# FFN joints: the first pair's gate and up products taken in turns, the final norm's stores issued by POOL, the weights' sums in five buffers

## The chip, the cores and the metric

The kernel runs on one core of a Trainium2 chip. The metric is the device time of one execution in microseconds, the median of several runs. TensorE (PE in the profile) multiplies; VectorE (DVE), ScalarE (ACT) and GpSimd (POOL) do the elementwise work; SyncE (SP) issues transfers. Each engine runs its own instructions strictly in their order and waits on semaphores of the others.

## What is computed

An encoder block of width 1024 over 2048 tokens and 16 meta tokens: neighbourhood attention and a gated DeltaNet side by side, an output projection, then the feed-forward part (FFN) with 2816 hidden columns and a final norm. Only the last lines of the reference matter here:

```python
h = h + jnp.concatenate([y_na, y_dn], axis=-1) @ w_out[l]
u = rmsnorm(h, g_ffn[l])
h = h + (jax.nn.silu(u @ w_gate[l]) * (u @ w_up[l])) @ w_down[l]
...
return rmsnorm(h, g_final)[:, N_META:]
```

Everything is float32. On the chip each factor is split into a high and a low part (hi is the value rounded by a cast on ACT, lo the rest, subtracted on DVE), and a product is hi·hi + hi·lo + lo·hi.

## The kernel before, in words

All of the change lies in `phase_c`. Its first part (lines 1290 to 1434) multiplies by `w_out`, adds the residual, norms each of 16 token tiles and transposes it (`finish`, L1399). The FFN follows in two blocks of 1024 tokens. A block is `gate_up(blk)` and then `down(blk)`.

**Gate and up.** The hidden columns are taken in 11 pairs of column tiles. For each pair there are two rounds, n even for gate and n odd for up, so 22 rounds, and each is a 2 by 2 block product done in the seven products of Strassen and Winograd in place of eight. The right-hand operands of the seven, called by their roles, depend only on the tokens:

```python
    ROLES = ("B11", "T2", "T3", "T1", "B21", "T4", "B22")
    RESIDENT = 4
```

B11 to B22 are quarters of the block's transposed tokens, T1 to T4 sums of them made on POOL (L1416). The first four roles stay in SBUF (pool `u2`, called the residents below). The last three are written to DRAM (`S.ut`, name `ut`) and brought back when `gate_up` begins: `fetch` (L1454) loads each in two halves of 512 KB into the two raw buffers of pool `rawT` (name `rt`, L1451), and `hilo` (L1364) splits each half, ACT's cast at L1365 and DVE's subtraction at L1366. In block 1 the first of the three, B21, is loaded during `down(0)` already (`refill`, L1640).

The left-hand operands are the weights. `weights(n)` (L1461) loads two raw tiles (`rw`; pool `raw_a` for gate, `raw_b` for up), makes four sums s1 to s4 on POOL (name `s`, L1472, pool `sC` of four buffers) and splits seven operands into tiles of pool `w4C` (name `w4`, eight buffers). `gate_up` runs over

```python
            seq = [(n, i) for n in range(NFF) for i in range(7)]
```

with the operands prepared seven products ahead (`AHEAD`). A product is 12 matmuls of 128x512 (L1521) into a PSUM tile `pg`; DVE adds it out of PSUM to tiles `eg` (gate) or `eu` (up) at L1533, ACT applies silu to gate (L1537), and DVE multiplies by up and SP stores the result to `hd` (L1541, L1542). In block 0, `finish` of the last token tile runs inside `gate_up` (`before`, at i == 1): eight transposes (L1408), sums (L1416) and stores to `ut` (L1422).

**Down.** `down(blk)` (L1568) multiplies by `w_down` in two halves of four token tiles (L1593). At the end of a half, `leave(j)` (L1600) norms each tile: DVE adds the residual into `o` (L1607), ACT squares (L1608), DVE makes the reciprocal root (L58 to L64), ACT scales (L1612), POOL multiplies by the gain `gvec` (L1613) and SP stores 512 KB (L1614). The last half of all goes another way; the other three halves make 12 such stores.

A **joint** is the place where a block's `gate_up` begins: the first behind the `w_out` products, the second behind `down(0)`. The order on each engine is not the order of this code: a scheduler that simulates the program moves instructions forward and back within the limits of their data and buffers.

Of the kernel before, what the change touches and what calls it, by code (L numbers as in the profile page):

```python
# [8 lines left out]
F32 = mybir.dt.float32  # L9
# [3 lines left out]
ALU = mybir.AluOpType  # L13
# [3 lines left out]
P = 128  # L17
# [3 lines left out]
D = 1024  # L21
# [25 lines left out]
def bc(ap, shape):  # L47
    return ap.to_broadcast(shape)
# [1241 lines left out]
def phase_c(tc, S, W, wes, x, w_out, g_ffn, w_gate, w_up, w_down, g_final, out):  # L1290
# [6 lines left out]

    nc = tc.nc
    NFF = 22
    ROLES = ("B11", "T2", "T3", "T1", "B21", "T4", "B22")  # L1300
    RESIDENT = 4
    with ExitStack() as ps_es:
        es = ExitStack()
# [16 lines left out]
        pd_ = ps_es.enter_context(tc.tile_pool(name="pdC", bufs=2, side="right", space=PSUM))  # L1320
# [22 lines left out]
        yT, hs, us, bt = {}, {}, {}, {}  # L1343
# [16 lines left out]
        pg_ = ps_es.enter_context(tc.tile_pool(name="pgC", bufs=4, space=PSUM))  # L1360
# [38 lines left out]
        def finish(j, new):  # L1399

            u = us.pop(j)
            t = order[j]
            even = raw_t.tile([P, 2, 512], F32, name="rt") if t % 2 == 0 else None
            for hf in range(2):
                pt = pt_.tile([P, 4, P], F32, name="tp")
                for q in range(4):
                    k = hf * 4 + q
                    nc.tensor.transpose(pt[:, q], u[:, k * P:(k + 1) * P], S.ident)  # L1408
                b = even[:, hf].rearrange("p (q c) -> p q c", c=P) if t % 2 == 0 else new()
                nc.scalar.copy(b, pt)  # L1410
                bt[f"B{hf + 1}{t % 2 + 1}"] = b
            if t % 2 == 0:
                return
            for d, x0, x1 in (("T1", "B12", "B11"), ("T2", "B22", "T1"), ("T3", "B22", "B12"), ("T4", "B21", "T2")):
                bt[d] = new()
                nc.gpsimd.tensor_tensor(bt[d], bt[x0], bt[x1], ALU.subtract)  # L1416
            o = slice(t % 8 // 2 * P, (t % 8 // 2 + 1) * P)
            for i, r in enumerate(ROLES):
                if t < 8 and i < RESIDENT:
                    hilo(T[r][:, 0, :, o], T[r][:, 1, :, o], bt[r])  # L1420
                else:
                    nc.sync.dma_start(S.ut[t // 8, i, :, :, o], bt[r])  # L1422
            bt.clear()
# [12 lines left out]
        wes.close()  # L1436

        w4 = ps_es.enter_context(tc.tile_pool(name="w4C", bufs=8, side="right", reuse_waits="tile"))
        sp = ps_es.enter_context(tc.tile_pool(name="sC", bufs=4, side="right", reuse_waits="tile"))
        raw_b = ps_es.enter_context(tc.tile_pool(name="rawB", bufs=2, side="right", reuse_waits="tile"))  # L1440
        ev = ps_es.enter_context(tc.tile_pool(name="evC", bufs=7, side="right", reuse_waits="tile"))
        gl = ev.tile([P, D], F32, name="gvec", bufs=1)
        nc.sync.dma_start(gl, bc(g_final, [P, D]))

        ahead = {}

# [14 lines left out]
        def weights(n):  # L1461

            f, m = n // 2 * 2, n % 2
            raw = []
            for q in range(2):
                raw.append((raw_a, raw_b)[m].tile([P, KB, P], F32, name="rw"))
                nc.sync.dma_start(raw[q], (w_gate, w_up)[m][f + q])
            a11, a12, a21, a22 = (raw[i][:, 4 * j:4 * j + 4] for i in range(2) for j in range(2))

            def sum_(p, q, op):  # L1470
                s = sp.tile([P, 4, P], F32, name="s")
                nc.gpsimd.tensor_tensor(s, p, q, op)  # L1472
                return s

            def operand(src):
                w = w4.tile([P, 2, 4, P], F32R, name="w4")
                hilo(w[:, 0], w[:, 1], src)
                return w

            yield  # L1480
            s1 = sum_(a21, a22, ALU.add)
            s2 = sum_(s1, a11, ALU.subtract)
            yield operand(a11)
            yield operand(s2)
            s3 = sum_(a11, a21, ALU.subtract)
            s4 = sum_(a12, s2, ALU.subtract)
            yield operand(s3)
            yield operand(s1)
            yield operand(a12)
            yield operand(a22)  # L1490
            yield operand(s4)

        def gate_up(blk, before=None):


            AHEAD = 7
            gens = {n: weights(n) for n in range(NFF)}
            for n in range(2):
                next(gens[n])
            seq = [(n, i) for n in range(NFF) for i in range(7)]  # L1500
            made = {}

            def prepare(i):
                if i < len(seq):
                    n, p = seq[i]
                    made[i] = next(gens[n])
                    if p == 6 and n + 2 < NFF:
                        next(gens[n + 2])

            for i in range(AHEAD):  # L1510
                prepare(i)
            V = {}
            for i, (n, p) in enumerate(seq):
                if p == 0:
                    v = V[n % 2] = {}
                gate = n % 2 == 0
                ps = pg_.tile([P, 512], F32, name="pg")
                w, t = made.pop(i), T[ROLES[p]]
                for k in range(4):
                    for a, b in ((0, 0), (0, 1), (1, 0)):  # L1520
                        nc.tensor.matmul(ps, w[:, a, k], t[:, b, k], start=(k == 0 and (a, b) == (0, 0)), stop=(k == 3 and a == 1))  # L1521
                prepare(i + AHEAD)
                if i == 1:
                    if before:
                        before(lambda: ev.tile([P, 4, P], F32, name="eu", bufs=5) if len(bt) < 5 else ev.tile([P, 4, P], F32, name="eg"))
                    for r in ROLES[RESIDENT:]:
                        fetch(r, blk)

                def new():
                    return ev.tile([P, 512], F32, name="eg") if gate else ev.tile([P, 512], F32, name="eu", bufs=5)  # L1530

                def add(dst, x0):
                    nc.vector.tensor_tensor(dst, ps, x0, ALU.add)  # L1533

                def done(c, q, half):
                    if gate:
                        nc.scalar.activation(c, c, AF.Silu)  # L1537
                        V[q, half] = c
                    else:
                        h = V.pop((q, half))  # L1540
                        nc.vector.tensor_tensor(h, c, h, ALU.mult)  # L1541
                        nc.sync.dma_start(S.h[blk, n - 1 + q, :, half, :], h)  # L1542

                if p == 0:
                    v["u1"] = new()
                    nc.scalar.copy(v["u1"], ps)
                elif p == 1:
                    v["u2"] = new()
                    add(v["u2"], v["u1"])
                elif p == 2:  # L1550
                    v["u3"] = new()
                    add(v["u3"], v["u2"])
                elif p == 3:
                    c = new()
                    add(c, v["u3"])
                    add(v["u2"], v["u2"])
                    done(c, 1, 1)
                elif p == 4:
                    add(v["u1"], v["u1"])
                    done(v["u1"], 0, 0)  # L1560
                elif p == 5:
                    add(v["u3"], v["u3"])
                    done(v["u3"], 1, 0)
                else:
                    add(v["u2"], v["u2"])
                    done(v["u2"], 0, 1)

        def down(blk, hp, others, last):  # L1568
# [3 lines left out]
            for half in range(2):  # L1572
# [27 lines left out]
                def leave(j):  # L1600
                    o = o_[j]
                    t = blk * 8 + j * 2 + half
                    rows = slice(t * P, (t + 1) * P)
# [7 lines left out]
                    if not (last and half):  # L1611
                        nc.scalar.activation(o, o, AF.Copy, scale=rs)  # L1612
                        nc.gpsimd.tensor_tensor(o, o, gl, ALU.mult)  # L1613
                        nc.sync.dma_start(out[rows, :], o)  # L1614
                        return
                    for hf in range(2):
                        cs = slice(hf * 512, hf * 512 + 512)
# [30 lines left out]
        for blk in range(2):  # L1648
            with tc.tile_pool(name="u2b", bufs=1, reuse_waits="tile") as upb:
                for r in ROLES[RESIDENT:]:  # L1650
                    T[r] = upb.tile([P, 2, 4, 512], F32R, name=r)
                gate_up(blk, None if blk else lambda new: finish(15, new))
            if blk == 0:
                with tc.tile_pool(name="dC", bufs=3, reuse_waits="tile") as hp:
                    again = refill(1)
                    down(0, hp, again, False)
                    for _ in again:
                        pass
# [154 lines left out]
```

## Time and profile before

| | us |
|---|---|
| median of 3 runs | 2960.21 |
| lowest and highest run | 2955.19, 2973.32 |
| the profiled execution | 2969.27 |
| its span, first to last instruction | 2967.6 |
| TensorE busy in it | 2769.5 (93%) |

The profile is one execution recorded by the hardware. Times in its rows count from the start of the span. A row of the timeline shows start, duration, engine, line, operation, and in brackets how long the engine had been idle and which instruction released it. Names such as `B<-rt` are output and input; tiles of one name read alike, so `B` stands for B11, B21 and B22, and `T` for T1 to T4.

### The profile page before, as it was taken

Reading aid. Unit: us, or ns where it says so; the run is one execution under the profiler, and the core shown is the slowest. Engines: PE = TensorE matmul, PEld = TensorE weight load, DVE = VectorE, ACT = ScalarE, POOL = GpSimd, SP = SyncE. Lnnn points to the kernel's source line nnn. Section 1 sums busy time; section 2 is a strip of 40 time slices with the busy share of each in tenths; the row PEclk is TensorE's granted clock in tenths of the full one; section 3 lists DMA queues with packets and bytes.
Section 4 is the critical chain, followed back from the end, with each engine's and each line's share of the span. In section 5 each row is a group of like instructions: output and inputs, shape, how many; then the busy total and the mean of one; then the engine's idle time right before and its main releaser. Section 6 shows DMA issues by size and latency. Waiting matters only on the chain.

```text
span 2967.6 us, 45891 instructions
## 1 busy us (share of the span) xinstructions
PE 2769.5 (93%) x16364; PEld 2417.6 (81%) x16364; DVE 1735.3 (58%) x3908; ACT 1176.2 (40%) x2741; POOL 730.1 (25%) x757
## 2 busy tenths in 40 slices
PE   8899889889798998979998999999998999999998
PEld 8898889888798898868886888887886888888886
DVE  5895766586563556774566555555547555554354
ACT  5653324452324666752233333333434233333342
POOL 2343434141321112241234222210003222220010
PEclk9999999999999998979998999999998999999999
DMA  4675644575669988985535222237353222225452
GB/s 157 191 193 144 178 134 118 149 192 139 187 150 276 292 250 232 310 257 166 182 122 161 85 86 79 67 115 250 131 188 107 79 78 85 83 73 203 139 175 81
DMA packets 398018, 466.33 MB, mean 157 GB/s; under 512 B 91955, under 2 KB 302220, under 8 KB 396222
## 3 DMA queue, kind: packets, MB, share of 16 engines
q1 hardware_dynamic: 397790, 463.40, 51.8%
q8 instruction: 130, 2.13, 0.3%
q14 instruction: 98, 0.80, 0.1%
HBM read 334.14 MB, written 141.15 MB: 160 GB/s over the span
## 4 chain that ended last, share of the span: by engine, by line
PE 52%; DVE 3%; DMA 3%; ACT 1%; POOL 1%; issue 1%; SPq 0%; DVEq 0%; ACTq 0%; POOLq 0%
PE pg L1521 28%; PE pg L1593 8%; PE pd L1382 6%; PE pd L1593 4%; PE tp L1593 4%; DMA rt<-ut 1%; PE y L1062 1%; PE tp L1335 1%; DVE w L1366 1%; DMA b<-in_rel_dram 0%; PE tp L1408 0%; DMA k<-kx 0%; DVE z L1199 0%; DMA z<-zx 0%; PE y L1048 0%
## 5 line engine op out<-in xcount | busy, mean ns | idle before, releaser
L1521 PE MATMUL pg<-T,w 128*128 128x512 f32 x2112 | 512.7, 398 | 3.4 <-DVE T L1366 2.0
L1521 PEld LDWEIGHTS pg<-T,w 128*128 128x128 f32 x2112 | 398.8, 189 | 102.7 <-DVE T L1366 3.3
L346 PE MATMUL acc<-uh,wf 128*128 128x384 f32 (+5 forms) x1920 | 469.4, 330 | 1.2 <-ACT uh L288 1.2
L1521 PE MATMUL pg<-B,w 128*128 128x512 f32 x1584 | 394.4, 402 | 25.8 <-ACT B L1365 21.1
L1365 ACT CAST w<-rw 128x512 fp32r<-128x512 f32 x308 | 190.3, 620 | 518.9 <-PE tp L1593 253.7
L1521 PEld LDWEIGHTS pg<-B,w 128*128 128x128 f32 x1584 | 301.7, 191 | 103.1 <-ACT B L1365 23.5
L1366 DVE TENSOR_TENSOR w<-rw,w 128x512 fp32r<-128x512 f32 x308 | 225.1, 733 | 248.1 <-ACT w L1365 247.3
L346 PEld LDWEIGHTS acc<-uh,wf 128*128 128x128 f32 x1920 | 342.8, 194 | 3.8 <-ACT uh L288 1.3
L346 PE MATMUL acc<-ul,wf 128*128 128x384 f32 (+5 forms) x960 | 315.5, 329 | 0.0
L1593 PE MATMUL pg<-w,hT 128*128 128x512 f32 x1056 | 260.7, 395 | 1.6 <-ACT hT L1365 1.6
L1593 PEld LDWEIGHTS pg<-w,hT 128*128 128x128 f32 x1056 | 198.2, 188 | 50.1 <-ACT hT L1365 2.0
L370 PE MATMUL acc<-wn,uh 128*128 128x256 f32 (+3 forms) x1056 | 205.0, 292 | 0.2 <-ACT uh L288 0.2
L1365 ACT CAST w<-s 128x512 fp32r<-128x512 f32 x176 | 108.9, 621 | 241.6 <-PE pg L1521 233.7
L1533 DVE TENSOR_TENSOR eg<-pg,eg 128x512 f32<-128x512 f32 x154 | 104.3, 689 | 162.4 <-PE pg L1521 162.3
L1472 POOL TENSOR_TENSOR s<-rw 128x512 f32<-128x512 f32 x88 | 119.0, 1352 | 318.4 <-DVE w L1366 227.8
L346 PEld LDWEIGHTS acc<-ul,wf 128*128 128x128 f32 x960 | 186.0, 194 | 1.5 <-DVE ul L289 0.2
L1366 DVE TENSOR_TENSOR w<-s,w 128x512 fp32r<-128x512 f32 x176 | 129.8, 738 | 91.5 <-ACT w L1365 89.8
L1533 DVE TENSOR_TENSOR eu<-pg,eu 128x512 f32<-128x512 f32 x154 | 104.3, 690 | 115.4 <-PE pg L1521 115.4
L370 PEld LDWEIGHTS acc<-wn,uh 128*128 128x128 f32 (+1 forms) x1056 | 168.4, 192 | 2.3 <-ACT uh L288 0.5
L1382 PE MATMUL pd<-w,yh 128*128 128x512 f32 x512 | 160.9, 396 | 0.0
L370 PE MATMUL acc<-wn,ul 128*128 128x256 f32 (+3 forms) x528 | 155.2, 294 | 2.4 <-DVE rx_i L58 2.4
L440 DVE SCALAR_TENSOR_TENSOR ct<-cr,cw,ct 128x1024 f32<-128x1024 f32 (+1 forms) x96 | 140.4, 1468 | 25.1 <-ACT ct L438 24.2
(343 smaller groups left out, 5047.3 us busy)
## 6 DMA issues: line engine op xcount, KB each, us to landing
rw<-in_w_down_dram SPq DMA_DIRECT2D x88, 512.0 KB
rw<-in_w_gate_dram SPq DMA_DIRECT2D x44, 512.0 KB
rw<-in_w_up_dram SPq DMA_DIRECT2D x44, 512.0 KB
hd<-eg SPq DMA_DIRECT2D x88, 256.0 KB
s<-hd SPq DMA_DIRECT2D x88, 256.0 KB
raw<-in_w_feat_dram SPq DMA_DIRECT2D x80, 256.0 KB
w<-dx SPq DMA_DIRECT2D x24, 768.0 KB
xq<-xq SPq DMA_DIRECT2D x32, 512.0 KB
```

The costliest lines, as they stand in the source:

```text
L346: nc.tensor.matmul(ps[:, 0:c1 - c0], hl[:, a, k, :], (U.h, U.l)[l][ci][:, k, c0:c1], start=(i == 0), stop=(i == 23))
L370: nc.tensor.matmul(ps[0:np_, 0:n], (U.h, U.l)[l][ci][:, k, off:off + np_], hl[:, a, k, 0:n], start=(i == 0), stop=(i == 23))
L440: nc.vector.scalar_tensor_tensor(tt, raw[:, j:j + T], cw[:, b, j:j + 1], tt, op0=ALU.mult, op1=ALU.add)
L1062: nc.tensor.matmul(po, t.pT[0:w, c], t.v[0:w, c], start=(c == 0), stop=(c == nch - 1))
L1335: nc.tensor.transpose(pt[:, q], src[:, k * P:(k + 1) * P], S.ident)
L1365: nc.scalar.copy(dst_h, src)
L1366: eng.tensor_tensor(dst_l, src, dst_h, ALU.subtract)
L1382: nc.tensor.matmul(ps, (yh, yl)[a][:, k], wo[k][:, b, cs], start=(i == 0), stop=(i == 23))
L1472: nc.gpsimd.tensor_tensor(s, p, q, op)
L1521: nc.tensor.matmul(ps, w[:, a, k], t[:, b, k], start=(k == 0 and (a, b) == (0, 0)), stop=(k == 3 and a == 1))
L1533: nc.vector.tensor_tensor(dst, ps, x0, ALU.add)
L1593: nc.tensor.matmul(acc[j][hf], hk[f][:, a, j * P:(j + 1) * P], wk[f][hf][:, b], start=(f == 0 and i == 0), stop=(f == NFF - 1 and i == 2))
```

## The change

- `seq` takes the first gate round and the first up round in turns: two products of gate, two of up, then one of each. All later pairs stay as they were.
- T1 and T3 change places in ROLES, and the weights' operands follow. T1's product is kept in PSUM (a tile of pool `pd_`) and added out one product later, together with T3's.
- s4 is written in place over s2 by POOL; pool `sC` has five buffers in place of four. T3 is written in place over B12.
- In block 0 the last tile's `finish` and the fetches are issued at i == 2, and two of its tiles use the room of the gain vector, which is loaded after `gate_up(0)`.
- The final norm's 12 stores are issued by POOL in place of SP.

```diff
-    ROLES = ("B11", "T2", "T3", "T1", "B21", "T4", "B22")
+    ROLES = ("B11", "T2", "T1", "T3", "B21", "T4", "B22")
...
-                bt[d] = new()
+                bt[d] = bt["B12"] if d == "T3" else new()
...
-        sp = ps_es.enter_context(tc.tile_pool(name="sC", bufs=4, side="right", reuse_waits="tile"))
+        sp = ps_es.enter_context(tc.tile_pool(name="sC", bufs=5, side="right", reuse_waits="tile"))
...
-        gl = ev.tile([P, D], F32, name="gvec", bufs=1)
-        nc.sync.dma_start(gl, bc(g_final, [P, D]))
...
             yield operand(s2)
+            yield operand(s1)
             s3 = sum_(a11, a21, ALU.subtract)
-            s4 = sum_(a12, s2, ALU.subtract)
             yield operand(s3)
-            yield operand(s1)
+            nc.gpsimd.tensor_tensor(s2, a12, s2, ALU.subtract)
             yield operand(a12)
             yield operand(a22)
-            yield operand(s4)
+            yield operand(s2)
...
-            seq = [(n, i) for n in range(NFF) for i in range(7)]
+            seq = [(0, 0), (0, 1), (1, 0), (1, 1)] + [(n, i) for i in range(2, 7) for n in range(2)]
+            seq += [(n, i) for n in range(2, NFF) for i in range(7)]
...
-                ps = pg_.tile([P, 512], F32, name="pg")
+                ps = pd_.tile([P, 512], F32, name="pd") if p == 2 else pg_.tile([P, 512], F32, name="pg")
...
-                if i == 1:
+                if i == 2:
                     if before:
-                        before(lambda: ev.tile([P, 4, P], F32, name="eu", bufs=5) if len(bt) < 5 else ev.tile([P, 4, P], F32, name="eg"))
+                        g = ev.tile([P, 2, 4, P], F32, name="gvec", bufs=1)
+                        places = [g[:, 0], g[:, 1]]
+                        before(lambda: places.pop() if places else ev.tile([P, 4, P], F32, name="eg"))
...
                 elif p == 2:
+                    v["p5"] = ps
+                elif p == 3:
                     v["u3"] = new()
                     add(v["u3"], v["u2"])
-                elif p == 3:
+                    ps = v["p5"]
                     c = new()
                     add(c, v["u3"])
...
-                        nc.sync.dma_start(out[rows, :], o)
+                        nc.gpsimd.dma_start(out[rows, :], o)
...
             if blk == 0:
+                gl = ev.tile([P, D], F32, name="gvec", bufs=1)
+                nc.sync.dma_start(gl, bc(g_final, [P, D]))
```

How the order on the engines moves, at three places. First TensorE at the first joint of the kernel before: `w4_...` are weight operands, B and T the roles, `pg_...` the products' PSUM tiles, `tp_...` the transposes of the last token tile.

```order
L1521 MATMUL pg_17997<-B11_16172,w4_17968 128x512 x12
L1521 MATMUL pg_18019<-T2_16173,w4_17971 128x512 x12
L1521 MATMUL pg_18090<-T3_16174,w4_17978 128x512 x2
L1521 MATMUL pg_18112<-T1_16175,w4_17981 128x512 x2
L1521 MATMUL pg_18090<-T3_16174,w4_17978 128x512 x10
L1521 MATMUL pg_18112<-T1_16175,w4_17981 128x512 x9
L1408 MATMUL tp_18035<-ident_102,rt_17913 128x128 x4
L1408 MATMUL tp_18042<-ident_102,rt_17913 128x128 x4
L1521 MATMUL pg_18112<-T1_16175,w4_17981 128x512
L1521 MATMUL pg_18132<-B21_17953,w4_17984 128x512 x12
```

The same engine and place with the change, from the first product to the transposes:

```order
L1522 MATMUL pg_17986<-B11_16172,w4_17959 128x512 x12
L1522 MATMUL pg_18006<-T2_16173,w4_17962 128x512 x2
L1522 MATMUL pg_18025<-B11_16172,w4_17969 128x512 x2
L1522 MATMUL pg_18006<-T2_16173,w4_17962 128x512 x10
L1522 MATMUL pg_18025<-B11_16172,w4_17969 128x512 x10
L1408 MATMUL tp_18043<-ident_102,rt_17906 128x128 x4
L1408 MATMUL tp_18049<-ident_102,rt_17906 128x128 x4
```

Behind the transposes come T2, T1 and T3 for both rounds, and then, with the last two resident products at its head:

```order
L1522 MATMUL pg_18149<-T3_16175,w4_17983 128x512 x12
L1522 MATMUL pg_18175<-T3_16175,w4_18001 128x512 x12
L1522 MATMUL pg_18202<-B21_17944,w4_18020 128x512 x6
L1522 MATMUL pg_18220<-B21_17944,w4_18039 128x512 x6
L1522 MATMUL pg_18202<-B21_17944,w4_18020 128x512
L1522 MATMUL pg_18220<-B21_17944,w4_18039 128x512
L1522 MATMUL pg_18239<-T4_17945,w4_18108 128x512
```

The transposes stand behind 36 matmuls instead of 47, and the first matmul on B21 behind eight products instead of four.

Next SP at the first joint, from the last weight load that both share to B21's second load; `rt<-ut` are the fetches, `rw` the weights. Before:

```order
L1443 DMA gvec_17948<-in_g_final_dram 128x1024
L1467 DMA rw_17993<-in_w_gate_dram 128x1024
L1467 DMA rw_17995<-in_w_gate_dram 128x1024
L1451 DMA rt_18064<-ut_90 128x1024
L1422 DMA ut_90<-eu_18047 512x1x128
L1422 DMA ut_90<-eu_18049 512x1x128
L1467 DMA rw_18184<-in_w_up_dram 128x1024
L1422 DMA ut_90<-eg_18051 512x1x128
L1451 DMA rt_18066<-ut_90 128x1024
```

With the change:

```order
L1449 DMA rt_18069<-ut_90 128x1024
L1422 DMA ut_90<-gvec_18042 512x1x128
L1422 DMA ut_90<-eg_18055 512x1x128
L1422 DMA ut_90<-eg_18057 512x1x128
L1465 DMA rw_18145<-in_w_gate_dram 128x1024
L1465 DMA rw_18165<-in_w_up_dram 128x1024
L1422 DMA ut_90<-gvec_18042 512x1x128
L1465 DMA rw_18147<-in_w_gate_dram 128x1024
L1449 DMA rt_18071<-ut_90 128x1024
```

The gain vector and the second gate round's weights leave their place ahead of B21's first load, and three weight loads, in place of one, stand between B21's two.

Last POOL at the second joint; `o` are the final norm's tiles, `s` the weights' sums. Before:

```order
L1472 TENSOR_TENSOR s_23090<-rw_23042 128x512
L1613 TENSOR_TENSOR o_22470<-o_22470,gvec_17948 128x1024
L1472 TENSOR_TENSOR s_23092<-s_23090,rw_23040 128x512
L1613 TENSOR_TENSOR o_22509<-o_22509,gvec_17948 128x1024
L1472 TENSOR_TENSOR s_23150<-rw_23040,rw_23042 128x512
L1472 TENSOR_TENSOR s_23152<-rw_23040,s_23092 128x512
L1613 TENSOR_TENSOR o_22548<-o_22548,gvec_17948 128x1024
L1472 TENSOR_TENSOR s_23250<-rw_23075 128x512
L1613 TENSOR_TENSOR o_22587<-o_22587,gvec_17948 128x1024
```

With the change (L1619 are the stores):

```order
L1618 TENSOR_TENSOR o_22439<-o_22439,gvec_21101 128x1024
L1619 DMA out_0_dram<-o_22439 128x1024
L1618 TENSOR_TENSOR o_22478<-o_22478,gvec_21101 128x1024
L1486 TENSOR_TENSOR s_23025<-rw_23009,s_23025 128x512
L1619 DMA out_0_dram<-o_22478 128x1024
L1470 TENSOR_TENSOR s_23057<-rw_23009,rw_23011 128x512
L1618 TENSOR_TENSOR o_22517<-o_22517,gvec_21101 128x1024
L1619 DMA out_0_dram<-o_22517 128x1024
L1618 TENSOR_TENSOR o_22556<-o_22556,gvec_21101 128x1024
L1619 DMA out_0_dram<-o_22556 128x1024
L1470 TENSOR_TENSOR s_23215<-rw_23174 128x512
L1470 TENSOR_TENSOR s_23217<-s_23215,rw_23172 128x512
```

The four stores now stand in POOL's queue, each behind its multiply, and the sums for the second pair (s_23215, s_23217) behind all of them.

## Rows read from the trace of the kernel before

**Rows 1.** The page, the chain that ended last: share of the span by line.

```profile
PE pg L1521 28%; PE pg L1593 8%; PE pd L1382 6%; PE pd L1593 4%; PE tp L1593 4%; DMA rt<-ut 1%; PE y L1062 1%; PE tp L1335 1%; DVE w L1366 1%; DMA b<-in_rel_dram 0%; PE tp L1408 0%; DMA k<-kx 0%; DVE z L1199 0%; DMA z<-zx 0%; PE y L1048 0%
```

**Rows 2.** Windows: us, PE busy (matmuls), granted clock, DMA share, GB/s.

```profile
1555.50:1600.00 44.50, 29.19 (x103) 0.81 0.69 220
1600.00:2011.70 411.70, 411.69 (x1758) 1.00 0.29 89
2259.70:2298.00 38.30, 24.47 (x85) 0.78 0.45 151
1559.80:1568.00 8.20, 8.20 (x37) 1.00 0.98 340
```

**Rows 3.** Timeline of PE in the body: start, us, row.

```profile
1707.89 2.97 PE L1521 MATMUL pg<-B,w 128*128 128x512 f32 x12
...
1727.58 2.97 PE L1521 MATMUL pg<-B,w 128*128 128x512 f32 x12
```

**Rows 4.** Timeline of PE, the first joint and the end of its block.

```profile
1555.55 0.71 PE L1521 MATMUL pg<-B,w 128*128 128x512 f32 x2
...
1567.99 1.03 PE L1408 MATMUL tp<-ident,rt 128*128 128x128 f32 x8
...
2013.25 1.67 PE L1593 MATMUL pg<-w,hT 128*128 128x512 f32 x6 [1.55 <-ACT hT L1365]
```

**Rows 5.** Timeline of PE, the second joint and the end of its block.

```profile
2259.75 2.96 PE L1521 MATMUL pg<-B,w 128*128 128x512 f32 x12
...
2281.60 0.79 PE L1521 MATMUL pg<-B,w 128*128 128x512 f32 x1 [10.45 <-ACT B L1365]
...
2711.36 0.86 PE L1593 MATMUL pg<-w,hT 128*128 128x512 f32 x3
```

**Rows 6.** Waits of PE from 1555 to 1612: us in total, times, longest.

```profile
PE pg L1521 <- ACT B L1365: 10.4, 3, 4.4
...
PE pg L1521 <- DVE ss L1325: 1.1, 1, 1.1
```

**Rows 7.** Timeline of ACT in the second joint.

```profile
2280.51 1.98 ACT L1365 CAST B<-rt 128x1024 fp32r<-128x1024 f32 x2
```

**Rows 8.** Timeline of SP in the first joint: issues of transfers.

```profile
1569.05 0.33 SPq L1451 DMA_DIRECT2D rt<-ut  x1
...
1576.42 0.33 SPq L1451 DMA_DIRECT2D rt<-ut  x1
```

**Rows 9.** Timeline of ACT in the first joint.

```profile
1581.98 1.04 ACT L1365 CAST B<-rt 128x1024 fp32r<-128x1024 f32 x1 [2.86 <-DMA rt<-ut]
1585.66 1.04 ACT L1365 CAST T<-rt 128x1024 fp32r<-128x1024 f32 x1 [2.63 <-DMA rt<-ut]
...
1595.54 1.04 ACT L1365 CAST B<-rt 128x1024 fp32r<-128x1024 f32 x1 [1.27 <-DMA rt<-ut]
```

**Rows 10.** The line of the final norm's stores: ns min/median/max, first and last start.

```profile
L1614 SPq DMA_DIRECT2D out_dram<-o x12: 343/382/846, 2151.3 to 2857.0; - x12
```

**Rows 11.** Timeline of POOL in the second joint.

```profile
2270.64 2.35 POOL L1613 TENSOR_TENSOR o<-o,gvec 128x1024 f32<-128x1024 f32 x1 [2.21 <-ACT o L1612]
...
2276.45 2.34 POOL L1613 TENSOR_TENSOR o<-o,gvec 128x1024 f32<-128x1024 f32 x1 [2.25 <-ACT o L1612]
```

**Rows 12.** Timeline of POOL in the first joint.

```profile
1561.41 4.61 POOL L1472 TENSOR_TENSOR s<-rw 128x512 f32<-128x512 f32 x1 [2.97 <-DVE w L1366]
```

**Rows 13.** Timeline of DVE in the second joint.

```profile
2270.64 2.37 DVE L63 SCALAR_TENSOR_TENSOR rf_t<-rs,rf_t 128x1 f32<-128x1 f32 x1
...
2274.68 0.21 DVE L63 SCALAR_TENSOR_TENSOR rf_t<-rs,rf_t 128x1 f32<-128x1 f32 x1
...
2289.28 1.23 DVE L1366 TENSOR_TENSOR T<-rt,T 128x1024 fp32r<-128x1024 f32 x1 [4.76 <-ACT T L1365]
```

**Rows 14.** Timeline of POOL and ACT in the body.

```profile
1662.27 1.29 POOL L1472 TENSOR_TENSOR s<-rw 128x512 f32<-128x512 f32 x1 [4.44 <-DVE w L1366]
...
1654.73 0.62 ACT L1365 CAST w<-s 128x512 fp32r<-128x512 f32 x1 [2.20 <-PE pg L1521]
```

More of the change, by code (lines that the diff above doesn't have):

```diff
@@ L1514, in gate_up @@
                 if p == 0:
-                    v = V[n % 2] = {}
+                    V[n % 2] = {}
+                v = V[n % 2]
                 gate = n % 2 == 0
-                ps = pg_.tile([P, 512], F32, name="pg")
+                ps = pd_.tile([P, 512], F32, name="pd") if p == 2 else pg_.tile([P, 512], F32, name="pg")
                 w, t = made.pop(i), T[ROLES[p]]
```

## The prediction, made before the changed kernel ran

> **What bounds the kernel now.** I read the chain that ended last first: the largest of its lines by far are the FFN's gate and up products, L1521, with 28% of the span [rows 1]. A change around L1521 pays only where TensorE stands still there, so the windows by stage come next [rows 2]: in the body of a block (1600 to 2011.7) TensorE is busy for 411.69 of 411.70 us at full granted clock. In the two stretches in which a block begins (the joints) it is busy 29.19 of 44.50 us at a clock of 0.81, and 24.47 of 38.30 us at 0.78. All there is to win lies in the joints.
>
> How much that is: in the body, seven products begin at 1707.89 and the next seven at 1727.58 [rows 3], 2.813 us a product; a block's 154 products need 433.2 us. In the first block they run from 1555.55 to 2011.70 (down's first matmul at 2013.25 has an idle time of 1.55 before it), with eight transposes of some 0.9 us between [rows 4]: 456.15 - 433.2 - 0.9 = **22.05 us lost**. In the second they run from 2259.75 to 2711.36 [rows 5]: 451.6 - 433.2 = **18.4 us lost**. Together 40.45 us, waits and matmuls at a low clock both. In the first joint 44.50 - 29.19 = 15.3 of the 22.05 are waits [rows 2], so a microsecond of wait costs about 1.45 in the end.
>
> What ends the waits: in the first joint three on ACT's cast of B21 or B22, 10.4 us, and one of 1.1 us on DVE's norm chain [rows 6]; in the second one single wait of 10.45 us for the cast of B21 [rows 5]. TensorE has four operands in SBUF (B11, T2, T3, T1), so one set of four products, 11.25 us, then wants B21. In the second joint that cast comes at 2280.51 [rows 7] while the resident products end at 2259.75 + 11.25 = 2271.0. In the first its chain is a load at 1569.05, right after the transposes (1567.99) that free its buffer, a second load at 1576.42, its cast at 1581.98, and so on through two buffers to B22's last cast at 1595.54 [rows 4, 8, 9].
>
> **The change part by part.** *Gate and up of the first pair in turns.* Eight products instead of four need nothing but residents: 22.5 us of work stand ahead of B21, 11.25 more than before in each joint. No matmul is added or removed. I replay each joint with the durations of before.
>
> First joint. Demand: start 1555.55, plus 22.5, plus the 1.1 of wait (nothing in the change touches it), plus 0.9 of transposes: residents end at 1580.0. In the new order TensorE takes the first halves of B21 for both products (12 matmuls, 2.8 us), so B21's second half is wanted at 1582.9, T4's first at 1583.4, B22's second near 1597. Supply: the transposes stand behind 36 matmuls instead of 47; 11 of 0.234 us make 2.6 us, and the chain hangs on them. SP now puts three weight loads between B21's two loads where one stood, two more of 512 KB: at the 340 GB/s of a stretch in which the queues were full [rows 2] 3.1 us if they are full, nothing if not; I take 1, since over the joint they moved 220 [rows 2]. That moves the chain by 1.6: B21's second cast ends at 1581.4 (in time), T4's first, 1585.66 before [rows 9], ends at 1584.06 + 1.04 = 1585.1 (1.7 late), B22's last at 1595.0 (in time). Left of the 22.05: 1.1 + 1.7 x 1.45 = **3.6 us**. The bounds: 1.1 if T4 is in time; and, with the chain not shifted at all (T4's cast ends 1586.7, 3.3 late) and the 3.1 on top, 1.1 + 6.4 x 1.45 = 10.4 us.
>
> Second joint. Residents end at 2259.75 + 22.5 = 2282.3. B21 was loaded during down; its two casts (1.98 us together) stood on ACT behind a silu of the fourth product [rows 7]. In the new order they stand behind the cast for the fourteenth weight operand, which waits for a buffer that the sixth product gives back at 2276.6: casts about 2277.2 to 2279.2, low parts by 2280.7, in time. That frees the two raw buffers, so T4's loads go at about 2279.5 and its cast comes at 2284.3, wanted at 2287.9; B22 at 2290.2, wanted at 2293.8. Left: **1.0 us** for what a replay misses, with 0 below.
>
> *Stores of the final norm on POOL.* Twelve issues leave SP, 0.38 us each [rows 10]; SP stands idle most of the time, so this alone is worth nothing. On POOL they stand between the gain multiplies (2.35 us [rows 11]) and the weights' sums; behind the joint's four stores wait the sums for the second pair, then on ACT the cast of one of these, then T4's cast. T4 and B22 also lie where the norm's tiles lay, so their first write waits until the stores have landed. No transfer in the trace is issued by POOL. Bounds for one: 0.34 us as the shortest on SP [rows 10], and 4.61 us, a sum of POOL beside a busy DVE [rows 12]; I take 1.3, the undisturbed sum of 1.29 [rows 14], because it is the usual row. The multiplies come 5.8 us apart [rows 11], so three stores fit between them and the fourth is issued by about 2280.1 and landed 5.6 us later (the longest way from load to cast, 1576.42 to 1581.98 [rows 8, 9]) at 2285.7: 2.2 us ahead of T4's demand. With 4.61 it lands near 2291.4 (the stores before it overrun their gaps by 1.2 each), T4's cast of 1.04 ends at 2292.4, 4.5 late, and twice that if B22 follows: 9 us, the upper bound of this joint. The other eight stores stand in the middle of a down phase, where TensorE wants nothing of POOL.
>
> The Trainium skill ("SBUF — State Buffer", section "SBUF: two separate sides") speaks against this edit: descriptors of a transfer that GpSimd issues are written by its own cores, which are locked out while DVE holds the shared port; it gives about 0.62 us alone and 3.1 us overlapped. Four times 3.1 are, as an estimate from that page, 12.4 us of POOL; the fourth store would land at 2287.5 and the sum would come out 1 to 2 us higher. The trace has such a lock, seen from DVE's side: an operation on 128x1 took 2.37 us beside a gain multiply of 2.35 that began at the same time, and 0.21 the next time [rows 11, 13].
>
> *Sum in place, T1 before T3, five buffers, T1's product held in the other PSUM pool.* Counts of sums, casts and evictions stay. In the body the in-place sum waits until DVE has read s2; that is the second operand of a round and the result the seventh, five products or 14.1 us later, less three sums of 1.29: about 10 us of slack. The casts of the body wait for TensorE to give back a buffer (2.20 us before the one at 1654.73) and POOL idles 4.44 us before a sum [rows 14]: that is the cover. Cost 0, up to the price in the slower rival. T3 in place and the late load of the gain vector: 0, since POOL's subtractions end well before T4 is fetched, and the vector is first used in down.
>
> **Sum.** 40.45 - 3.6 - 1.0 - 0 = 35.9 us gained, on the profiled 2969.27: 2933.4. The median of 2960.21 lies 9.1 below the profiled execution; the same microseconds there give **2924.3**.
>
> **The rivals.** *A: the fetch chain binds the first joint.* B21, T4 and B22 pass through two raw buffers; if the loads crowd behind the weights, the joint keeps the 10.4 us of above and another 3.1 x 1.45 at B22, 14.9 instead of 3.6: 2935.6. For it: 340 GB/s at the joint's start [rows 2]. Against: most steps of the chain wait for a buffer or the cast, not for bytes.
>
> *B: POOL's stores wait for DVE.* If a store cannot be issued while DVE works, all go when DVE falls idle, near 2284.5 (it idles 4.76 us before 2289.28 [rows 13]); four of 1.3 and 5.6 to land make 2295.3 against T4's 2287.9: 7.4 late, 10.7 with the low clock: 2934. Against: POOL's sum beside a busy DVE became slower, it did not wait for DVE's idle time [rows 12]. That is the page's lock made a mechanism of this joint.
>
> *C: the wait only moves*, TensorE stopping as long at T4 as it did at B21: within a few us of 2960. Against: B22's last half is cast at 1595.5 even before [rows 9], and is wanted near 1597.
>
> *D, slower: the in-place sum reaches TensorE in every round.* Should POOL's sum come too late for the last operand, a round loses one sum and one cast, 1.29 + 0.62 = 1.9 us; the 40 rounds behind the first pairs make 76: 3000. It cancels the gain from 0.9 us a round, and is slower by over 1% from 1.64 us. Against: the 10 us of slack.
>
> **How the numbers follow.** One per cent, 29.6 us, is about what a measurement tells from no change; faster means below 2930.6. Forecast 0.60, A 0.17, B 0.11, C 0.06, D 0.06. Losses of 1.1 to 19.4 us (10.4 and 9) give 2920.9 to 2939.2; the runs of before spread by -5 to +13 around their median, and 7 to 9 on either side give 2912 to 2946, which takes in A and B. Faster by over 1%: nine tenths of the forecast and a quarter of A and B, 0.61; slower 0.06 from D; the rest, 0.33, within 1%.
>
> **What would show it.** In the trace after: TensorE without a gap from the transposes until near 1580 and from 2259 to 2282, at full clock; the wait for B's cast gone in the second joint; in the first at most 2 to 3 us, at T4; 154 products in about 437 and 434 us; POOL's stores about 1 us each. Wrong if a wait of over 5 us on T's or B's cast stays in either joint, if POOL's stores keep it from its sums, or if seven products of the body take more than 19.69 us.

## The result, and the profile after

The changed kernel takes 2934.08 us, the median of 6 runs from 2932.37 to 2942.55; the kernel before, run beside it, 2965.04 (6 runs, 2955.19 to 2973.32). The ratio is 0.9904, with a 95% interval of 0.988 to 0.9927: about 31 us or 1.0% less, where the forecast said 35.9. The profiled execution took 2934.77 us with a span of 2933.1.

The windows of TensorE of the changed kernel by stage come first (columns: stretch, us, PE busy, granted clock, DMA share, GB/s). They answer to [rows 2].

```profile
1551.20:1576.50 25.30, 24.21 (x108) 1.00 0.62 181
1576.50:1582.00 5.50, 2.94 (x13) 1.00 1.02 352
1582.00:1592.20 10.20, 8.62 (x25) 0.67 0.66 236
...
1600.00:1994.00 394.00, 394.00 (x1684) 1.00 0.28 91
2242.50:2282.00 39.50, 38.90 (x165) 1.00 0.43 157
2282.00:2676.50 394.50, 394.50 (x1685) 1.00 0.28 92
```

The second joint (2242.5 to 2282) is busy for 38.90 of 39.50 us, at full clock. The body is as full as before, so the edits to the sums cost nothing there. Most of what is left of waiting stands between 1576.5 and 1592.2, at the end of it at a clock of 0.67. The timeline of TensorE at the first joint and at the end of its block, as [rows 4]:

```profile
1551.20 0.71 PE L1522 MATMUL pg<-B,w 128*128 128x512 f32 x2
...
1582.32 0.73 PE L1522 MATMUL pg<-B,w 128*128 128x512 f32 x2 [2.88 <-ACT B L1365]
1584.31 1.22 PE L1522 MATMUL pg<-T,w 128*128 128x512 f32 x2 [1.27 <-ACT T L1365]
1585.33 4.47 PE L1522 MATMUL pg<-B,w 128*128 128x512 f32 x10
...
1995.63 1.67 PE L1598 MATMUL pg<-w,hT 128*128 128x512 f32 x6 [1.28 <-ACT hT L1365]
```

And at the second joint, as [rows 5]:

```profile
2242.54 2.97 PE L1522 MATMUL pg<-B,w 128*128 128x512 f32 x12
...
2271.88 3.07 PE L1522 MATMUL pg<-T,w 128*128 128x512 f32 x12 [0.60 <-DVE T L1366]
...
2676.56 0.86 PE L1598 MATMUL pg<-w,hT 128*128 128x512 f32 x3
```

Measured as in the prediction, the first joint loses 1995.63 - 1.28 - 1551.20 - 434.1 = 9.05 us (22.05 before), and the second 2676.56 - 2242.54 - 433.2 = 0.8 us (18.4 before): 30.6 us gained, which is the measured difference. The span fell by 34.5 us; the other 4 lie ahead of the FFN, which began at 1551.20 instead of 1555.55. They lie ahead of the first product with `w_out` as well (1347.5 instead of 1351.9), where nothing was moved, and in the traces below the FFN begins anywhere from 1539.2 to 1552.8, so that part is not shown to be a gain.

The same two sums, from each trace (us lost by TensorE), and the time from the FFN's first product to the end of the span, which takes in what the joints leave out:

| kernel | first joint | second joint | FFN to the end, us | median, us | ratio to before (95%) |
|---|---|---|---|---|---|
| before | 22.05 | 18.4 | 1412.0 | | |
| changed | 9.05 | 0.8 | 1381.9 | 2934.08 | 0.9904 (0.988 to 0.9927) |
| e1, turns undone | 22.6 | 16.7 | 1411.6 | 2960.42 | 0.9991 (0.9977 to 1.0005) |
| e2, stores on SP | 9.1 | 1.2 | 1382.6 | 2930.52 | 0.9892 (0.9868 to 0.9916) |
| e4, third raw buffer | 8.0 | 1.3 | 1381.4 | 2933.48 | 0.9892 (0.9867 to 0.9916) |
| e5, token sums on DVE | 9.5 | 0.35 | 1381.4 | 2932.21 | 0.9891 (0.9867 to 0.9915) |
| e6, e5 and fetches by POOL | 11.7 | 6.0 | 1388.0 | 2942.3 | 0.9942 (0.9927 to 0.9958) |
| e7, e4 and e5 | 3.95 | 1.7 | 1378.9 | 2926.31 | 0.9887 (0.9868 to 0.9906) |
| e8, e7 and fetches by POOL | 5.9 | 10.4 | 1388.1 | 2941.84 | 0.9937 (0.9923 to 0.9952) |
| e9, e5 and fetches by ACT | 10.2 | 0.65 | 1386.1 | 2938.37 | 0.9929 (0.9911 to 0.9947) |
| e10, e7 and stores on SP | 3.8 | 5.0 | 1381.8 | 2931.5 | 0.9897 (0.9871 to 0.9923) |
| e11, changed again | 9.0 | 0.1 | 1380.5 | 2930.39 | 0.9893 (0.9868 to 0.9918) |

The losses of a joint repeat within about 1 us (changed, e2 and e11); the FFN's time repeats within about 2 us, and the whole times scatter by several us, so differences of a few us between these kernels are read from the joints and from the FFN's time.

**Why the first joint keeps 9 us.** The issues of SP, then DVE, then ACT of the changed kernel between the transposes and the wait:

```profile
1561.68 0.33 SPq L1449 DMA_DIRECT2D rt<-ut  x1
...
1574.04 0.33 SPq L1465 DMA_DIRECT2D rw<-in_w_gate_dram  x1
1575.17 0.33 SPq L1449 DMA_DIRECT2D rt<-ut  x1
```

```profile
1562.09 6.80 DVE L1366 TENSOR_TENSOR w<-s,w 128x512 fp32r<-128x512 f32 x5 [2.48 <-ACT w L1365]
...
1569.41 4.59 DVE L1366 TENSOR_TENSOR w<-rw,w 128x512 fp32r<-128x512 f32 x3
1573.93 1.21 DVE L1366 TENSOR_TENSOR B<-rt,B 128x1024 fp32r<-128x1024 f32 x1
```

```profile
1568.76 1.04 ACT L1365 CAST B<-rt 128x1024 fp32r<-128x1024 f32 x1
...
1581.22 1.05 ACT L1365 CAST B<-rt 128x1024 fp32r<-128x1024 f32 x1 [1.80 <-DMA rt<-ut]
```

Counted from the joint's first product, B21's first load goes at 10.5 us instead of 13.5 [rows 8], as forecast. But its second load goes at 24.0 instead of 20.9, and its second cast comes at 30.0 instead of 26.4 [rows 8, 9]. The second load takes the buffer of the first half, and that is free only when DVE has taken the low part (1573.93 plus 1.21; the load goes at 1575.17). DVE reaches it late, since two rounds' weights are split at once and each split is slow there: five low parts in 6.80 us and three in 4.59, where one takes 0.68 undisturbed, while POOL works beside. From 1562.09 to the end of B21's low part DVE has no gap of over 0.2 us. The first half's cast had not gained from the earlier load either: it comes 17.6 us after the first product, and 17.05 before the change, since it stands on ACT behind the weights' casts. Once the second load goes, it needs 6.0 us to its cast (5.6 before), with the second pair's weights and the gain vector issued around it; the window from 1576.5 shows the DMA engines full at 352 GB/s.

### The profile page after: what moved, and what is told of

It is laid out like the page before. It is cut to its first block, busy times and chain, and to the rows that moved or that the text cites. A ratio compares the mean times of both kernels' runs of the same rounds, so it can differ in the third digit from the quotient of the medians.

```text
span 2933.1 us, 45808 instructions
## 1 busy us (share of the span) xinstructions
PE 2763.0 (94%) x16364; PEld 2415.5 (82%) x16364; DVE 1765.8 (60%) x3908; ACT 1173.4 (40%) x2741; POOL 744.6 (25%) x769
## 4 chain that ended last, share of the span: by engine, by line
PE 52%; DVE 3%; DMA 2%; issue 1%; ACT 0%; POOL 0%; SPq 0%; DVEq 0%; ACTq 0%; POOLq 0%
PE pg L1522 24%; PE pg L1598 8%; PE pd L1382 6%; PE pd L1598 4%; PE tp L1598 4%; PE pd L1522 4%; DMA rt<-ut 1%; PE y L1062 1%; PE tp L1335 1%; DVE w L1366 0%; PE tp L1408 0%; DMA b<-in_rel_dram 0%; DVE z L1199 0%; DMA k<-kx 0%; DMA z<-zx 0%
## 5 line engine op out<-in xcount | busy, mean ns | idle before, releaser
L1366 DVE TENSOR_TENSOR w<-rw,w 128x512 fp32r<-128x512 f32 x308 | 245.4, 799 | 253.2 <-ACT w L1365 252.1
L1522 PE MATMUL pg<-T,w 128*128 128x512 f32 x1584 | 394.0, 397 | 2.3 <-ACT T L1365 1.3
L1522 PEld LDWEIGHTS pg<-T,w 128*128 128x128 f32 x1584 | 298.4, 189 | 76.5 <-ACT T L1365 1.7
L440 DVE SCALAR_TENSOR_TENSOR ct<-cr,cw,ct 128x1024 f32<-128x1024 f32 (+1 forms) x96 | 140.4, 1467 | 24.6 <-ACT ct L438 23.8
L175 POOL TENSOR_TENSOR wf<-raw,wf 128x512 fp32r<-128x512 f32 x80 | 109.4, 1381 | 164.1 <-ACT wf L174 160.5
L1536 DVE TENSOR_TENSOR eg<-pg,eg 128x512 f32<-128x512 f32 x110 | 75.9, 690 | 106.0 <-PE pg L1522 106.0
```

The costliest lines, as they stand in the source:

```text
L175: nc.gpsimd.tensor_tensor(lo, raw, hi, ALU.subtract)
L440: nc.vector.scalar_tensor_tensor(tt, raw[:, j:j + T], cw[:, b, j:j + 1], tt, op0=ALU.mult, op1=ALU.add)
L1366: eng.tensor_tensor(dst_l, src, dst_h, ALU.subtract)
```

## The experiments

**e1: the turns undone.** The rest of the change stays.

```diff
-            seq = [(0, 0), (0, 1), (1, 0), (1, 1)] + [(n, i) for i in range(2, 7) for n in range(2)]
-            seq += [(n, i) for n in range(2, NFF) for i in range(7)]
+            seq = [(n, i) for n in range(NFF) for i in range(7)]
```

> The changed kernel with its old sequence of products (one gate round, then one up round); all other edits stay. Theory (the turns carry the whole gain): the first joint loses about 22 us again and the second about 18, as in the kernel before, so this kernel is 30 us slower than the changed one and equal to the one before (ratio 0.997 to 1.003). Rival (the other edits carry part of it, the stores on POOL above all): the second joint loses less than 12 us, and the ratio to before is under 0.997.

Its time is that of before, and both joints lose what they lost there. TensorE's wait for B21's cast at the second joint is back, though the stores are issued by POOL and the buffers are five:

```profile
2267.18 0.80 PE L1521 MATMUL pg<-B,w 128*128 128x512 f32 x1 [8.12 <-ACT B L1365]
```

So the turns carry the gain. The other edits by themselves bring nothing that the time shows. They are meant to make room for the turns; what the turns would bring without them, no run shows.

**e2: the stores back on SP.**

```diff
-                        nc.gpsimd.dma_start(out[rows, :], o)
+                        nc.sync.dma_start(out[rows, :], o)
```

> The changed kernel with the final norm's stores issued by SP again. Theory (the stores' engine is worth nothing): TensorE still loses about 1 us at the second joint and about 9 at the first, time within 3 us of the changed kernel. Rival (stores on SP hold the loads of T4 and B22 behind them while they wait for POOL's multiplies): a wait of 2 to 6 us for T or B at the second joint.

Both joints are as in the changed kernel, and the longest wait at the second is 1.17 us, for a low part of T4. In this order of work the engine that issues the stores is worth nothing that shows.

**e4: a third raw buffer; e5: the last tile's token sums on DVE.** In e4 every third half goes through a buffer of its own:

```diff
-        w4 = ps_es.enter_context(tc.tile_pool(name="w4C", bufs=8, side="right", reuse_waits="tile"))
+        w4 = ps_es.enter_context(tc.tile_pool(name="w4C", bufs=7, side="right", reuse_waits="tile"))
+        raw_u = ps_es.enter_context(tc.tile_pool(name="rawU", bufs=1, side="right", reuse_waits="tile"))
...
-                raw = raw_t.tile([P, 2, 512], F32, name="rt")
+                pool = raw_u if turn[0] % 3 == 1 else raw_t
+                turn[0] += 1
+                raw = pool.tile([P, 2, 512], F32, name="rt")
```

> The changed kernel with a third raw buffer for the fetches of B21, T4 and B22, and seven weight operands in place of eight to make room. Theory (what is left at the first joint, 8.9 us, comes of two raw buffers: B21's second load waits until DVE has taken the low part of the first half): the second load goes within 3 us of the first, no wait for B21 is left, and the joint loses 2 to 5 us instead of 8.9; 4 to 7 us faster than the changed kernel. Rival (the transfers themselves bind, they move 352 GB/s there): the loads only crowd, T4 and B22 come as late as before, and the joint loses 7 us or more.

In e5:

```diff
-                nc.gpsimd.tensor_tensor(bt[d], bt[x0], bt[x1], ALU.subtract)
+                (nc.vector if j == 15 else nc.gpsimd).tensor_tensor(bt[d], bt[x0], bt[x1], ALU.subtract)
```

> The changed kernel with the four token sums of the last tile (T1 to T4 inside the first joint) taken by DVE in place of POOL. Theory (DVE is slow there because POOL works beside it: eight low parts took 11.4 us where 0.68 each would be 5.4): four sums of 0.7 us come to DVE and 6 us of stretching go, B21's first low part comes about 3 us earlier, and the first joint loses 5 to 7 us instead of 8.9. Rival (DVE is simply full): the low part comes later and the joint loses 10 us or more.

Each mended its own link and left the joint nearly as it was. Of e4, SP's issues of fetches, ACT's cast of T4's second half, DVE's last low part of B22 and TensorE's last wait:

```profile
1549.53 0.98 SPq L1453 DMA_DIRECT2D rt<-ut  x1
...
1558.73 1.05 SPq L1453 DMA_DIRECT2D rt<-ut  x2
...
1575.96 1.30 SPq L1453 DMA_DIRECT2D rt<-ut  x2
...
1581.99 1.05 ACT L1365 CAST T<-rt 128x1024 fp32r<-128x1024 f32 x1 [2.69 <-DMA rt<-ut]
...
1590.67 2.28 DVE L1366 TENSOR_TENSOR B<-rt,B 128x1024 fp32r<-128x1024 f32 x1
...
1593.01 6.94 PE L1526 MATMUL pg<-B,w 128*128 128x512 f32 x22 [2.58 <-DVE B L1366]
```

The new buffer holds nothing of the last token tiles, so one half of B21 is loaded into it at 1549.53, ahead of the transposes; two more loads go together at 1558.73, and no wait for B21 is left. (So e4 takes away the wait for the transposes as well as the one for DVE's low part.) But T4's second half, issued at 1575.96 behind three weight loads, is cast at 1581.99, and TensorE now waits 2.58 us for B22's low part. There it is not the transfer that is late: the last half of B22 had been cast by 1587.39, and DVE came to it at 1590.67 and took 2.28 us, where 1.21 is usual. Of e5, SP's loads, DVE's last token sum and its three weight low parts, ACT's cast of T4, and TensorE:

```profile
1569.74 0.61 SPq L1449 DMA_DIRECT2D rt<-ut  x1
...
1573.04 0.60 SPq L1449 DMA_DIRECT2D rt<-ut  x1
...
1568.42 0.68 DVE L1416 TENSOR_TENSOR eg<-rt,eg 128x512 f32<-128x512 f32 x1
...
1569.63 1.89 DVE L1366 TENSOR_TENSOR w<-rw,w 128x512 fp32r<-128x512 f32 x3
...
1583.17 1.04 ACT L1365 CAST T<-rt 128x1024 fp32r<-128x1024 f32 x1 [2.60 <-DMA rt<-ut]
...
1584.27 0.79 PE L1522 MATMUL pg<-T,w 128*128 128x512 f32 x2 [3.02 <-ACT T L1365]
1586.13 1.22 PE L1522 MATMUL pd<-T,w 128*128 128x512 f32 x2 [1.07 <-ACT w L1365]
```

The three low parts take 1.89 us where they took 4.59, so POOL beside DVE had stretched them. B21's second load goes at 20.1 us after the first product instead of 24.0, but not because of them: at 1569.74 B21's first low part has not begun (it comes at 21.8 us, only 0.9 earlier than in the changed kernel). The load takes the other raw buffer, which the last token sum (`eg<-rt,eg`) gives back, at 1569.10 on DVE where POOL ended it at 1573.46. T4's load, issued at 1573.04, is cast ten us later. The windows of e5 show what it met:

```profile
1570.00:1577.00 7.00, 7.00 (x31) 1.00 1.00 272
1577.00:1584.00 7.00, 4.24 (x17) 1.00 0.95 383
1584.00:1591.00 7.00, 5.66 (x14) 0.56 0.36 116
```

From 1570 to 1584 the DMA engines are full: gain vector, four weight loads and three fetches were issued within some 8 us, and T4 stands in the middle of them. The clock falls to 0.56 behind the wait. So more than one link is late by about the same: the raw buffers, which token sums and DVE's low parts give back late, and the crowd of transfers. With one mended, another holds TensorE.

**e7: both.**

> Third raw buffer (e4) and token sums on DVE (e5) together. By its order five of the six fetches are issued ahead of the gain vector and of the second pair's weights. Theory (two links in a row, the raw buffer that waits for a low part and then the crowd of transfers, each of which takes the other's place when it alone is mended): the first joint loses 2 to 5 us where e4 lost 8.0 and e5 9.5; time 4 to 6 us under e4. Rival (DVE is the limit, it was busy 45 of 49 us there in e4): the loss stays at 7 us or more, with waits on DVE's low parts.

```profile
1562.30 1.08 SPq L1453 DMA_DIRECT2D rt<-ut  x2
...
1572.49 0.33 SPq L1453 DMA_DIRECT2D rt<-ut  x1
...
1573.66 0.62 SPq L1453 DMA_DIRECT2D rt<-ut  x1
...
1596.23 3.55 PE L1526 MATMUL pg<-B,w 128*128 128x512 f32 x14 [1.10 <-DVE B L1366]
```

Five of the six fetches go ahead of the gain vector and the weights (both of T4's halves by 1573.66), and the longest wait left in the joint is 1.1 us for B22's low part. It loses 3.95 us against 8.0 and 9.5, so most of what the changed kernel kept there goes when both are mended, and not with either alone. Which part of the pair does it (the buffers, the load on DVE, or the order of the fetches that follows from them), no run takes apart. DVE is not the limit that the rival took it for (7 us or more). By time e7 is 7.8 us under the changed kernel's median, but the intervals of the ratios overlap; by the joints it is 4.2 us (5.65 lost against 9.85), and by the FFN's time 3.0, or 1.6 against e11, which is within the scatter.

**e6, e8, e9: the fetches issued by another engine,** to take them out of the queue with the weights.

```diff
-                nc.sync.dma_start(raw, S.ut[blk, ROLES.index(r), :, 2 * q:2 * q + 2, :])
+                nc.gpsimd.dma_start(raw, S.ut[blk, ROLES.index(r), :, 2 * q:2 * q + 2, :])
```

> The kernel with the token sums on DVE (e5), and the fetches of B21, T4 and B22 issued by POOL in place of SP, so that they no longer stand in one queue with the second pair's weights and the gain vector. Theory (transfers crowd: in e5 T4's first load was issued at 1573.04 and cast at 1583.17, behind gain vector and three weight loads, at 383 GB/s): T4's first load takes 3 to 6 us instead of 10, the wait of 3.0 us for T is gone, and the first joint loses 4 to 6 us instead of 9.5. Rival (POOL's order holds the loads and the sums against each other, or the engines are shared alike by all queues): the loss stays 8 us or grows.

> All three together: third raw buffer, token sums on DVE, fetches issued by POOL. If queue order was still a limit in e7, 1 to 3 us less than e7; if not, the same within 1 us at the first joint; if POOL's order hurts the weights' sums, a new wait on w or s of TensorE in the first joint.

e9 has `nc.scalar` in that place.

> As e6, but the fetches are issued by ACT. Theory (sharing the engines with the other queue brings T4 earlier): T4's first load takes 3 to 6 us as in e6. Rival (a load that waits for its raw buffer stops ACT's casts behind it): TensorE waits longer for ACT's casts at the joints, first joint over 10 us, second joint over 3 us.

None brought the gain that was looked for, and the losses of e6 (11.7 us) and e9 (10.2) at the first joint lie where their rivals had them. Of e6, POOL's fetches, its first sum for the second pair's weights, and TensorE:

```profile
1575.74 0.53 POOL L1449 DMA_DIRECT2D rt<-ut  x1 [4.19 <-DVE B L1366]
1581.74 0.53 POOL L1449 DMA_DIRECT2D rt<-ut  x1 [5.47 <-DVE B L1366]
1583.71 1.27 POOL L1470 TENSOR_TENSOR s<-rw 128x512 f32<-128x512 f32 x1 [1.45 <-DMA rw<-in_w_gate_dram]
...
1587.54 1.22 PE L1522 MATMUL pd<-T,w 128*128 128x512 f32 x2 [3.29 <-ACT w L1365]
```

POOL stops 4.19 and 5.47 us for DVE's low parts before it may overwrite a raw buffer, and the weights' sums stand behind; TensorE waits 3.29 us for a weight operand. But the same sum in e5, where POOL issues no fetch:

```profile
1581.96 1.26 POOL L1470 TENSOR_TENSOR s<-rw 128x512 f32<-128x512 f32 x1 [16.59 <-DVE eu L1536]
```

It starts 32.3 us after the first product in both, in e6 released last by its weight load, and TensorE takes the operand at 36.5 us in e5 (1586.13) and at 36.1 in e6. So POOL's stops did not make it later. The second pair's weights are a third link, about as late as the others, which the wait for T4 had covered in e5. e8 has no such wait at the first joint; it loses 1.9 us more than e7, with waits of 1.66 us for DVE's norm chain and of 1.62 and 1.46 for B22, which none of its three expectations had. At the second joint e6 loses 6.0 and e8 10.4 us, with T4 cast late (waits of 4.7 and 7.5 us). There POOL's order does hold a load: e6 issues T4's first at 2271.67, behind sums of which the first had waited 4.71 us for its weights. Of e9, one fetch by ACT, T4's cast and TensorE:

```profile
1573.86 0.33 ACTq L1449 DMA_DIRECT2D rt<-ut  x1
...
1581.18 1.04 ACT L1365 CAST T<-rt 128x1024 fp32r<-128x1024 f32 x1 [2.59 <-DMA rt<-ut]
...
1587.17 1.22 PE L1522 MATMUL pd<-T,w 128*128 128x512 f32 x2 [4.16 <-ACT w L1365]
```

T4's load still takes 7.3 us, and the wait has gone to the weight operand, 4.16 us. The joints lose only 1.0 us more than in e5, but the FFN takes 4.7 us more: among the rest, the first matmul of `down(0)` waits 3.26 us for ACT's cast of its operand (0.64 in e5), which the sums of the joints leave out. So the fetches cost least on SP here, by the FFN's time 4.7 us less than on ACT and 6.6 less than on POOL (e5, e9, e6). That nothing but other loads is held up there is a likely reason, not a shown one.

**e10: e7 with the stores on SP; e11: the changed kernel again.**

> e7 (third raw buffer, token sums on DVE) with the final norm's stores on SP again. If the stores' engine is worth nothing, as e2 said, the joints lose what they lost in e7 (about 4 and 2 us) and the time is that of e7 within 3 us: ratio to before 0.986 to 0.990. If SP's stores now hold the fetches of the second joint, the second joint loses 4 us or more.

> The changed kernel, not edited, beside e10 on one chip. If what the joints show is the whole gain (9.9 us lost in both together against 40.5 before, so 30.6 gained), its ratio to before is 0.988 to 0.991, 4 to 6 us above e10; if the stages ahead of the FFN gained too (4.35 us in the first trace), the ratio is 0.988 or less and its FFN begins earlier than before's in this trace again.

e11 repeats the joints of the changed kernel, and its ratio lies inside the expected band; it was to be 4 to 6 us above e10 and is 1.1 below. Its FFN begins at 1549.0, before's at 1555.55; but e1's, no faster than before, begins at 1539.2, so an early start tells nothing. e10 loses 5.0 us at the second joint where e7 loses 1.7:

```profile
2256.33 1.05 ACT L1365 CAST T<-rt 128x1024 fp32r<-128x1024 f32 x1 [5.10 <-DMA out_dram<-o]
...
2257.42 1.23 DVE L1366 TENSOR_TENSOR T<-rt,T 128x1024 fp32r<-128x1024 f32 x1 [3.01 <-ACT T L1365]
...
2261.07 2.85 PE L1526 MATMUL pg<-T,w 128*128 128x512 f32 x7 [2.11 <-DVE eg L1540]
```

This wait is on an eviction by DVE, not on a fetch that SP holds. In DVE's order the eviction (2260.24) stands behind T4's low part, which waited 3.01 us for T4's cast, and the cast had waited 5.10 us for a store of the final norm to land, since T4 lies where the norm's tiles lay. In e7 T4's first cast waits 3.38 us for a store too, but DVE has an eviction in front of its low part and stops only 0.60 us. Moving the stores changed the scheduler's order there. So "the stores' engine is worth nothing" holds for the changed kernel's order and not for every order.

## Why the prediction was right, and where it was off

*Direction, place and mechanism* held: both joints, nothing in the body, down or tail, by the eight resident products ahead of B21. The time, 2934.08, lies in the range, though not on the side held more likely: faster than 2930.6 had 0.61, and the band in which it lies 0.33. The forecast of 2924.3 was too low by 10, 5 of which are the kernel before itself (its median over more runs is 2965.04 instead of 2960.21) and 5 the first joint.

*The second joint* came out as replayed: 0.8 us against 1.0. From its first product on, the casts of B21 come at 17.6 us, forecast 17.5; T4's first cast at 25.8, forecast 24.6:

```profile
2260.13 2.00 ACT L1365 CAST B<-rt 128x1024 fp32r<-128x1024 f32 x2
...
2268.33 1.05 ACT L1365 CAST T<-rt 128x1024 fp32r<-128x1024 f32 x1
```

*The first joint* is the step that failed: "that moves the chain by 1.6". The transposes and the first load did come earlier, but the chain did not stay rigid behind them. I had shifted ACT's casts and left out the link between them, DVE's low part that frees the raw buffer, and DVE is just what the turns load: two rounds' weight operands are wanted in the same stretch. The rows had shown the link. Of the 15.3 us of waits in the first joint before, 3.7 ended on DVE's low parts, which the reading of [rows 6] passes over:

```profile
PE pg L1521 <- DVE B L1366: 2.5, 2, 2.0
PE pg L1521 <- DVE T L1366: 1.2, 1, 1.2
```

So does the reading of the second joint, where four smaller waits, 3.4 us together, follow the "one single wait" of 10.45. Instead of 1.6 us earlier, B21's second cast came 3.6 us later. I expected the wait at T4; it was 2.88 us at B21 and 1.27 at T4. The term was 3.6 and measured 9.05, inside its bounds of 1.1 to 10.4. The price of a wait was too low as well: waits of 5.2 us (0.63, 0.46, 2.88, 1.27) lost 9.05, 1.7 times and not 1.45, with the clock at 0.67 for some 10 us behind the wait. The 1.1 us of wait that the sum let stand for DVE's norm chain came out at 1.09, but on weight operands (0.63 and 0.46): luck in the size.

*The stores.* Twelve on POOL took 0.6 us each, and the transfers landed in 4.0 us (line of the stores: ns min/median/max; then us to landing):

```profile
L1619 POOL DMA_DIRECT2D out_dram<-o x12: 531/596/772, 2133.1 to 2819.9; - x12
...
DMA to landing us min/median/max: 2.9/4.0/8.4
```

I had taken 1.3 and 5.6. The first was on the safe side, the second was not for every store (the longest took 8.4); the sum took no harm, and e2 shows that the stores on POOL bring nothing either. Rival B fell: DVE was at work beside each of the twelve, and the longest held POOL for 0.77 us. The Trainium skill ("SBUF — State Buffer", section "SBUF: two separate sides") gives its 0.62 and 3.1 us for a whole transfer, the second beside a `tensor_copy` of DVE. Beside the twelve stores here DVE ran subtractions, additions and operations on 128x1 and no copy, so this case does not test that figure; the prediction had put it on POOL's time and on operations for which the Trainium skill does not give it.

*Rival A* was no rival but a part of the truth: the transfers do crowd, which shows once B21's load comes early (e5). *Rival C*, the moving wait, described e4 and e5. *Rival D* fell with the full body.

## What to carry to other kernels

When work is put ahead of a fetch, replay each link of the fetch, the engine that frees its buffer included, with the extra work that the same edit puts on that engine. If two links of a chain are late by about the same, mending one shows next to nothing (e4 and e5 against e7); mend both before judging either. In this kernel loads that wait for a buffer did best on SP's queue, and the joint did best with the loads wanted next ahead of the prefetches of weights (e7). When a sum of waits at two places is the measure, keep the time of the whole stage beside it: it showed 4.7 us of e9 where the joints showed 1.0.

## What was not expected of the hardware

DVE and POOL slow each other more than I had counted, with plain 128x512 operations: three low parts took 4.59 us beside POOL's token sums and 1.89 without them (e5). A transfer issued by POOL held POOL for only 0.53 to 0.77 us, beside a busy DVE too.
